# Four k-tiles of the second branch projection by seven products, two column blocks at a time

## The chip, the cores and the metric

The kernel runs on one core of a Trainium2 chip. The time is device microseconds of a whole execution, here the median of three runs. A profiled execution gives the trace. In its rows PE is TensorE's matmul, PEld its weight load, DVE VectorE, ACT ScalarE, POOL GpSimd, SP the engine that issues most loads. A line such as L109 is a line of the kernel file.

## The reference

One decoder layer on x of 256 rows and 2048 columns, all in float32:

- h = rmsnorm(x), then one projection into queries, keys and values of 16 heads of 128, and into three gates of 2048 columns each;
- three kinds of attention side by side: stick-breaking on 4 heads, block attention on 6, dilated attention on 6;
- the merge, which the change is about:

```python
merged = (gates[:, :, 0] * (flat(o_a) @ w_branch[:ea])
          + gates[:, :, 1] * (flat(o_b) @ w_branch[ea:eb])
          + gates[:, :, 2] * (flat(o_c) @ w_branch[eb:]))
x = x + merged @ w_out
```

- a second rmsnorm, a SwiGLU network of width 5632, and the residual.

## The kernel before

**Numbers in two parts.** Every float32 operand of a matmul is split into a high part in TensorE's reduced format and the remainder: `split` (L109) casts on ACT and subtracts on DVE. A product (`product`, L173 to L175) is three matmuls into the same PSUM bank: high x high, high x low, low x high. Activations are the stationary side (128 x 128), weights the moving side (128 x 512).

**Tiles.** Rows make two row tiles of 128; columns go by blocks of 512; the inner dimension by k-tiles of 128. A load fetches two k-tiles of one column block, 512 KB. Raw weights land in four `w_raw` buffers or in a pool called `gx`; their split parts lie in five pairs `w_hi` and `w_lo`. PSUM has eight banks: two of `ps`, two of `qs`, two for transposes (`tr`), and from the last gates on one each of `z` and `v`. `banks()` hands out `ps` and `qs` in turn.

**Plain and by sevens.** `project` (L133 on) multiplies k-tile after k-tile for one column block. `project_pair` (L358 on) does two column blocks at once, and for the chunks of four k-tiles in `acts.wc` it replaces eight block products (2 row tiles x 2 column blocks x 2 halves of k) by seven, as Winograd's form of Strassen's method does. The weights are then quarters b11, b12, b21, b22 of 512 KB and sums of them; the activations are four blocks and four sums of them, made by `put_sums` (four subtractions or additions, L227 to L232, and a split). The order is: form 1 into X, form 5 into Z, form 2 into Y, plain blocks of the second column block into Z and V, form 6, form 7, form 3, then the plain blocks of the first column block and form 4. With `by_banks` the bank X is copied to Y, and Z to V, on ACT; otherwise snapshots in SBUF serve. With `by_dma` the sum b12 + b22 is made by an accumulating transfer on POOL's queue, as u + b21 always is.

**The stages.** Input projection (pairs, chunks 0 and 1 by sevens), attention beside it, the branch projection, output projection, the second norm, the gate and up projection, the down projection. Work that hangs on a stage (transposes, splits, norms) is cut into steps in `stages`; `advance` runs one step at each weight block.

**The branch projection.** Column blocks c = 0 to 3, and in each the three branches with 4, 6 and 6 k-tiles, all by `project`. Behind each branch the gates, kept in DRAM, are multiplied with the banks (L988, L990) and added up (L991); their loads go by POOL (L977). After a column block, `to_m` transposes the merged rows, splits them into `m`, and for chunks 0 and 1 also makes the sums that the output projection wants. At the last branch the pools of the attention phase (`ph1`) are closed and the first output pair is begun.

**What sets the order.** A planner places the instructions of each engine, in the order in which they can start by its own timeline; those pinned by `keep_in_program_order` keep the written order. `fetch` (L106) pins loads on SP, `raw_weights` (L121) doesn't.

## Time and profile before

| | us |
|---|---|
| median of 3 runs | 1335.99 (1335.94 to 1340.19) |
| profiled execution | 1341.53 |
| its span | 1339.8 |
| TensorE busy | 1329.8 (99%) |
| VectorE busy | 1175.4 (88%) |
| ACT busy | 946.3 (71%) |
| GpSimd busy | 132.5 (10%) |
| mean granted TensorE clock | 0.999 |

A row of busy time adds up how long an engine's instructions lasted, and overlapping ones are counted once. A timeline row has start, duration, engine, line and operation, with output and inputs; in brackets stands idle time ahead of it and what ended it.

### The profile page before, as it was taken

Reading aid. Unit: us, or ns where it says so; the run is one execution under the profiler, and the core shown is the slowest. Engines: PE = TensorE matmul, PEld = TensorE weight load, DVE = VectorE, ACT = ScalarE, POOL = GpSimd, SP = SyncE. Lnnn points to the kernel's source line nnn. Section 1 sums busy time; section 2 is a strip of 40 time slices with the busy share of each in tenths; the row PEclk is TensorE's granted clock in tenths of the full one; section 3 lists DMA queues with packets and bytes.
Section 4 is the critical chain, followed back from the end, with each engine's and each line's share of the span. In section 5 each row is a group of like instructions: output and inputs, shape, how many; then the busy total and the mean of one; then the engine's idle time right before and its main releaser. Section 6 shows DMA issues by size and latency. Waiting matters only on the chain.

```text
span 1339.8 us, 17786 instructions
## 1 busy us (share of the span) xinstructions
PE 1329.8 (99%) x6237; PEld 1159.1 (87%) x6237; DVE 1175.4 (88%) x1261; ACT 946.3 (71%) x1216; POOL 132.5 (10%) x197
## 2 busy tenths in 40 slices
PE   9999999999999999999999999999999999999998
PEld 6888888888888888888888878888888888888887
DVE  7978898988888997988999979998889997998887
ACT  6786867788777776546877867777877776664563
POOL 1100110001110111110210000001000001001010
PEclk9999999999999999999999999999999999999999
DMA  9987878888788878888988799889899877789983
GB/s 356 307 281 246 264 211 255 256 271 227 264 263 282 289 230 287 299 283 278 283 296 273 255 232 272 234 263 306 278 295 272 264 226 259 244 278 299 275 270 95
DMA packets 119793, 355.75 MB, mean 266 GB/s; under 512 B 32864, under 2 KB 34584, under 8 KB 119704
## 3 DMA queue, kind: packets, MB, share of 16 engines
q1 hardware_dynamic: 77016, 277.45, 57.6%
q0 software_dynamic: 20272, 70.81, 23.2%
q10 hardware_dynamic: 22416, 6.36, 3.1%
q8 instruction: 49, 0.80, 0.2%
q14 instruction: 40, 0.33, 0.1%
HBM read 294.26 MB, written 14.70 MB: 231 GB/s over the span
## 4 chain that ended last, share of the span: by engine, by line
PE 93%; DMA 3%; issue 2%; DVE 1%; ACT 0%; SPq 0%; DVEq 0%; POOL 0%; POOLq 0%; ACTq 0%
PE qs L174 11%; PE qs L175 11%; PE qs L173 11%; PE ps L174 11%; PE ps L175 11%; PE ps L173 11%; PE z L173 4%; PE z L175 4%; PE z L174 4%; PE v L173 2%; PE v L175 2%; PE v L174 2%; DMA u<-g_raw 1%; PE tr L175 1%; PE tr L174 1%
## 5 line engine op out<-in xcount | busy, mean ns | idle before, releaser
L109 DVE TENSOR_TENSOR w_lo<-w_raw,w_hi 128x1024 fp32r<-128x1024 f32 x298 | 361.0, 1219 | 44.7 <-ACT w_hi L109 43.3
L109 ACT CAST w_hi<-w_raw 128x1024 fp32r<-128x1024 f32 x298 | 309.4, 1048 | 94.8 <-PE qs L175 28.1
L109 ACT CAST w_hi<-g_raw 128x1024 fp32r<-128x1024 f32 x220 | 227.1, 1050 | 106.7 <-PE qs L175 32.8
L109 DVE TENSOR_TENSOR w_lo<-g_raw,w_hi 128x1024 fp32r<-128x1024 f32 x220 | 262.2, 1219 | 19.5 <-ACT w_hi L109 17.1
L109 ACT CAST w_hi<-u 128x1024 fp32r<-128x1024 f32 x165 | 172.0, 1049 | 122.3 <-DVE u L1194 21.2
L109 DVE TENSOR_TENSOR w_lo<-u,w_hi 128x1024 fp32r<-128x1024 f32 x165 | 199.2, 1221 | 48.9 <-ACT w_hi L109 44.0
L174 PE MATMUL qs<-w_lo,h_hi 128*128 128x512 f32 x348 | 133.2, 383 | 3.2 <-DVE w_lo L109 3.2
L175 PE MATMUL qs<-w_hi,h_lo 128*128 128x512 f32 x348 | 132.6, 381 | 0.0
L174 PE MATMUL ps<-w_lo,h_hi 128*128 128x512 f32 x336 | 128.0, 381 | 0.5 <-DVE w_lo L109 0.5
L173 PE MATMUL qs<-w_hi,h_hi 128*128 128x512 f32 x348 | 128.1, 384 | 0.0
L175 PE MATMUL ps<-w_hi,h_lo 128*128 128x512 f32 x336 | 127.4, 380 | 0.1
L173 PE MATMUL ps<-w_hi,h_hi 128*128 128x512 f32 x336 | 123.1, 382 | 0.2 <-ACT h_hi L109 0.2
L402 POOL DMA_DIRECT2D u<-g_raw x47 | 40.9, 871 | 380.4 <-DVE w_lo L109 309.5
L174 PEld LDWEIGHTS qs<-w_lo,h_hi 128*128 128x128 f32 x348 | 66.1, 190 | 12.9 <-DVE w_lo L109 3.6
L173 PEld LDWEIGHTS qs<-w_hi,h_hi 128*128 128x128 f32 x348 | 66.1, 190 | 9.7 <-ACT sc L335 0.3
L175 PEld LDWEIGHTS qs<-w_hi,h_lo 128*128 128x128 f32 x348 | 66.1, 190 | 9.3
L174 PEld LDWEIGHTS ps<-w_lo,h_hi 128*128 128x128 f32 x336 | 63.5, 189 | 9.9 <-DVE w_lo L109 1.3
L175 PEld LDWEIGHTS ps<-w_hi,h_lo 128*128 128x128 f32 x336 | 63.5, 189 | 9.9 <-DVE h_lo L109 1.1
L173 PEld LDWEIGHTS ps<-w_hi,h_hi 128*128 128x128 f32 x336 | 63.3, 189 | 9.6 <-ACT h_hi L109 0.9
L351 DVE TENSOR_TENSOR u<-g_raw 128x1024 f32<-128x1024 f32 x47 | 57.2, 1219 | 14.5 <-DMA g_raw<-in_w_gu 11.3
L340 DVE TENSOR_TENSOR u<-u,g_raw 128x1024 f32<-128x1024 f32 x47 | 55.4, 1218 | 0.0
L396 POOL DMA_DIRECT2D g_raw<-g_raw x21 | 18.2, 864 | 254.6 <-DMA g_raw<-in_w_in 78.0
(440 smaller groups left out, 2978.1 us busy)
## 6 DMA issues: line engine op xcount, KB each, us to landing
w_raw<-in_w_in SPq DMA_DIRECT2D x103, 512.0 KB, 6.7
g_raw<-in_w_in SPq DMA_DIRECT2D x88, 512.0 KB, 6.3
g_raw<-in_w_gu SPq DMA_DIRECT2D x88, 512.0 KB, 6.0
w_raw<-in_w_gu SPq DMA_DIRECT2D x88, 512.0 KB, 6.6
w_raw<-in_w_down SPq DMA_DIRECT2D x56, 512.0 KB, 4.8
u<-g_raw POOLq DMA_DIRECT2D x51, 512.0 KB, 6.3
w_raw<-in_w_branch SPq DMA_DIRECT2D x32, 512.0 KB, 4.7
g_raw<-in_w_down SPq DMA_DIRECT2D x32, 512.0 KB, 5.2
```

Source lines behind the costliest of these rows:

```text
L109: cast, rest = nc.scalar.copy(hi, src), nc.vector.tensor_sub(lo, src, hi.bitcast(F32))
L173: nc.tensor.matmul(ps, ah, wh, start=start, stop=False, **how)
L174: nc.tensor.matmul(ps, ah, wl, start=False, stop=False, **how)
L175: nc.tensor.matmul(ps, al, wh, start=False, stop=stop, **how)
L340: tc.keep_in_program_order(nc.vector.tensor_add(d, d, a))
L351: nc.vector.tensor_add(d, a, b)
L396: nc.gpsimd.dma_start(d, a, accum_op=ALU.add)
L402: nc.gpsimd.dma_start(d, a, accum_op=ALU.add)
```

## The change

The loop over four column blocks becomes a loop over two pairs. In a pair the order is now: first branch of the second block; then `project_pair` for the second branch of both blocks, with k-tiles 4 to 7 (the first four of its six) by sevens and k-tiles 8 and 9 plain; inside it, after form 6, the first branch of the first block (`between`); then the third branch of both.

`project_pair` takes the list of plain k-tiles `ks` and the function `between`. With a single plain block per column it skips the plain blocks ahead of form 6, and the two banks of the first column block end with form 4. `by_banks` now holds for `w_branch` too.

The sums of heads 4 to 7, which the forms need, are made in place in `o_raw` at the end of the last gates, and split into a new pool `os`. For the second branch no new raw buffers are taken: the quarters b11, b12, b21, b22 lie in the slot of `h_hi` (the first norm's high parts), u and that branch's gates in the slot of `o_raw`, and the merged sums of the first pair in the slot of `h_lo`. `Slots` hands these out in order. The gates of the second branch are fetched at the beginning of a pair.

```diff
     def by_banks(w):
-        return w is w_gu or w is w_out
+        return w is not w_in
...
-        ks = [k for c in range(KT // 4) if c not in acts.wc for k in (4 * c, 4 * c + 2)]
+        ks = ks or [k for c in range(KT // 4) if c not in acts.wc for k in (4 * c, 4 * c + 2)]
+        split_at = (2, 3) if len(ks) > 2 else (0, len(ks))
...
-        rest(1, ks[2], Z, V)
+        if between:
+            between()
+        for k in ks[slice(*split_at)]:
+            rest(1, k, Z, V, stop=k == ks[-1])
...
-            rest(0, k, Y, X)
-        form(X, 4, u, False, False)
+            rest(0, k, Y, X, stop=k == ks[-1])
+        form(X, 4, u, False, len(ks) <= 2)
...
+        if k0:
+            for _ in range(2):
+                yield
+            heads_4_7 = o_raw[:, 4:8, :]
+            o_sums.put_sums(1, *(heads_4_7[:, :, t * P:(t + 1) * P] for t in range(NT)), heads_4_7)
...
-    for c in range(4):
-        ms = [half_kb() for _ in range(NT)]
-        for b, (k0, nk) in enumerate(((0, H_A), (H_A, H_B), (H_A + H_B, H_C))):
-            gt = [half_kb() for _ in range(NT)]
-            for t in range(NT):
-                nc.gpsimd.dma_start(gt[t], gate_mem[b, c, t])
-            ps = project(o, k0, w_branch, k0 * P, nk, c * NB)
...
+    def room(name):
+
+        return p1.tile([P, NH, S], F32, name=name).rearrange("p (n h) q -> p n (h q)", h=2 * NB // S)
...
+    kept = room("h_lo").rearrange("p n (t h) -> p n t h", t=NT)
+
+    for c in (0, 2):
+        if c:
+            ms = [[half_kb() for _ in range(NT)] for _ in range(2)]
+        else:
+            ms = [[kept[:, n, t] for t in range(NT)] for n in range(2)]
+        raws, other = room("h_hi"), room("o_raw")
+        gx = Slots((raws[:, 0], raws[:, 1], other[:, 0], raws[:, 2], raws[:, 3])[i].rearrange("p (k n) -> p k n", k=2) for i in range(5))
+        gts = [gates_of(1, c + n, [other[:, 2 + n, t * NB:(t + 1) * NB] for t in range(NT)]) for n in range(2)]
+        gated(0, ms[1], *branch(0, c + 1))
+        (a0, a1, _, _), _ = project_pair(o_sums, w_branch, c * NB, (c + 1) * NB, None, None, True,
+                                         lambda *b: gated(1, ms[1], gts[1], b), [H_A + 4],
+                                         lambda: gated(0, ms[0], *branch(0, c)))
+        turn.reverse()
+        gated(1, ms[0], gts[0], (a0, a1))
+        for n in range(2):
+            gt, ps = branch(2, c + n)
...
+            with behind_splits() if c + n == 3 else nullcontext():
+                gated(2, ms[n], gt, ps)
+            stages.append(to_m(c + n, ms[n]))
```

## The prediction

> **What bounds the kernel now.** I read the page's first part and its chain of waits, then busy times by stretch, then the instructions one by one where the changed stage begins and ends.

> ```profile
> span 1339.8 us, 17786 instructions
> PE 1329.8 (99%) x6237; PEld 1159.1 (87%) x6237; DVE 1175.4 (88%) x1261; ACT 946.3 (71%) x1216; POOL 132.5 (10%) x197
> PE 93%; DMA 3%; issue 2%; DVE 1%; ACT 0%; SPq 0%; DVEq 0%; POOL 0%; POOLq 0%; ACTq 0%
> ```

> TensorE is busy for 99% of the span and carries 93% of the chain that ended last, so work taken from it comes off the end, as long as the other engines keep it fed. The next fullest is VectorE, at 88%. The stage that changes is the projection of the three branches. In the timeline of TensorE it begins and ends here (columns: start, duration, engine, line, operation):

> ```profile
> 515.35 0.38 PE L173 MATMUL qs<-w_hi,o_hi 128*128 128x512 f32 x1
> ...
> 520.53 0.38 PE L173 MATMUL ps<-w_hi,o_hi 128*128 128x512 f32 x1
> ...
> 600.86 0.38 PE L173 MATMUL qs<-w_hi,m_hi 128*128 128x512 f32 x1
> ```

> The row at 515.35 is the first product of the attention output, the one at 600.86 the first of the output projection: the stage lasts 85.51 us. Between 515.35 and 520.53 lie the 24 matmuls of the first branch (4 k-tiles, 2 row tiles, 3 products each), so one costs 5.18 / 24 = 0.216 us from start to start, although its row says 0.38: each begins before the last has ended. The whole stage has 4 column blocks x 16 k-tiles x 2 x 3 = 384 of them. The chain of waits shows what else is in it:

> ```profile
> 542.06 0.87 PE tr L206 x8
> 563.66 0.87 PE tr L206 x8
> 585.26 0.87 PE tr L206 x8
> ```

> 384 x 0.216 + 3 x 0.87 = 85.55 us against 85.51: TensorE does not pause in this stage, and every matmul less is worth 0.216 us. What the other engines do meanwhile (columns: stretch, its length, then busy time and count of PE, weight loads, DVE, ACT, POOL, then clock and DMA):

> ```profile
> 515.35:600.86 85.51, 85.51 (x409) 75.06 (x408) 69.91 (x88) 45.58 (x52) 17.00 (x31) 1.00 0.87 305
> 540.00:580.00 40.00, 40.00 (x195) 35.16 (x194) 37.17 (x51) 21.63 (x28) 7.32 (x14) 1.00 0.83 277
> 601.00:641.00 40.00, 40.00 (x195) 35.16 (x194) 35.05 (x39) 24.13 (x31) 2.52 (x4) 1.00 0.79 264
> 641.00:690.00 49.00, 49.00 (x240) 43.09 (x240) 47.35 (x57) 39.62 (x61) 8.52 (x14) 1.00 0.95 301
> ```

> VectorE is busy for 69.91 of the 85.51 us, so it has 15.6 us to spare; in the two middle column blocks (540 to 580) only 2.8 of 40. After the stage it has 5.0 to spare in the 40 us of the first output pair and 1.7 in the next 49. TensorE is full in all four rows, the last with VectorE at 97%: nearly full is not yet too full.

> **What TensorE saves.** For each pair of column blocks, k-tiles 4 to 7 cost 4 x 2 blocks x 2 row tiles x 3 = 48 matmuls now; seven forms of 2 k-tiles and one row tile cost 7 x 2 x 3 = 42. Two pairs: 12 matmuls less, 12 x 0.216 = **2.6 us**. Loads do not change (four quarters replace four blocks, each 512 KB), nor do the transposes.

> [...]

> **What VectorE gets in exchange.** Its prices, again from start to start where it works without a gap:

> ```profile
> 522.71 3.50 DVE L109 TENSOR_TENSOR w_lo<-w_raw,w_hi 128x1024 fp32r<-128x1024 f32 x3 [1.28 <-ACT w_hi L109]
> ...
> 530.07 1.28 DVE L991 TENSOR_TENSOR sc<-sc 128x512 f32<-128x512 f32 x2
> ...
> 547.22 0.42 DVE L227 TENSOR_TENSOR sc<-sc 128x256 f32<-128x256 f32 x1
> 547.67 0.43 DVE L230 TENSOR_TENSOR sc<-sc 128x256 f32<-128x256 f32 x1
> ```

> Three of 1024 columns take 3.50 us with the last one's 1.22 us, so one per (3.50 - 1.22) / 2 = 1.14 us; two of 512 take 1.28 with the last one's 0.68, so one per 0.60; those of 256 follow at 0.45. Per pair the change adds three low-part splits (seven forms need seven weights, where four blocks needed four) and the two sums u = b11 + b12 and u + b22, each of 1024: 5 x 1.14 = 5.7. The differences c12 and c22, 512 each, add 2 x 0.60 = 1.2. That is 6.9 a pair and 13.8 for two. The sums of heads 4 to 7 add four of 256 and one split of 1024 once: 4 x 0.45 + 1.14 = 2.9. Together **16.7 us**. The gate products and their additions are as many as before.

> So VectorE would need 69.9 + 16.7 = 86.6 us in a stage for which TensorE needs only 85.5 - 2.6 = 82.9. The excess is **3.7 us**, more than the saving. It need not all fall on TensorE. The weight buffers hold five splits, so VectorE may enter the stage ahead and leave it with less in hand; the second chunk's sums in the merged columns (four of 0.45 and two splits of 0.60, 3.0 us) are used only in the second output pair; and 5.0 us are free right behind. Bounds on what stalls TensorE here: 0, if all of it slips into these 5.0 us, and 3.7, if none does.

> [...]

> **The start of the first pair.** Its raw quarters lie where the first norm's columns lay (h_hi), which the last product of the gates reads. That product starts just before 515.35, so these loads can only go then. They are pinned to the order of SP's queue, so what is pinned behind them waits too. What they take:

> ```profile
> L121 SPq DMA_DIRECT2D w_raw<-in_w_branch x32: 327/328/328, 500.0 to 579.2; - x32
> DMA to landing us min/median/max: 3.4/4.7/9.1
> ...
> L109 ACT CAST w_hi<-w_raw 128x1024 fp32r<-128x1024 f32 x31 | 32.4, 1050 | 35.2 <-PE ps L175 13.6 <-PE qs L175 11.3 <-DMA w_raw<-in_w_branch 8.9
> ...
> 515.55 0.69 DVE L431 TENSOR_TENSOR sc<-ps,sc 128x512 f32<-128x512 f32 x1 [0.28 <-PE ps L175]
> 516.16 1.22 DVE L109 TENSOR_TENSOR o_lo<-o_raw,o_hi 128x1024 fp32r<-128x1024 f32 x1
> ```

> The cover is the first branch of the other column block, put ahead of the pair: 5.18 us. A landing of 4.7, a cast of 1.05 and a low part of 1.22 make 6.97 us; the form's second matmul wants the low part at 5.18 + 0.22 = 5.40: 1.6 us late. At a landing of 3.4 it is 0.3 late, and work pulled forward from the other first branch (5.18 us more, free once two products of 0.60 have emptied its banks) can hide that. At 9.1 it is 6.0 late. Before this, VectorE still owes the two rows at 515.55 and 516.16 and the head sums, 0.6 + 1.14 + 2.9 = 4.6 us, and it needs u = b11 + b12 and a split right after. Bounds 0 and 6.0; I take **1.5**, near the median landing. VectorE catches up 1.5 us of its excess in this wait, so 2.2 of the 3.7 remain; I take about half, **1.2**, on TensorE, because the work that may slip (3.0 us) covers more than the remainder, but nothing orders it last.

> **What costs nothing.** ACT gets 6 casts of 1.05, one for the head sums, 4 bank copies and 4 snapshots of about 0.6, some 12 us, into a stage where it works 45.6 of 85.5 us. The accumulating transfers on POOL:

> ```profile
> 610.19 0.90 POOL L402 DMA_DIRECT2D u<-g_raw x1 [11.54 <-DVE w_lo L109]
> ...
> u<-g_raw POOLq DMA_DIRECT2D x51, 512.0 KB, 6.3
> ...
> 602.36 0.57 ACT L383 COPY qs<-qs 128x512 f32<-128x512 f32 x1 [1.85 <-PE qs L175]
> ```

> There are four more of them, 3.6 us of POOL's 68 idle ones, and each lands after about 6.3 us. Form 7 and form 4, which want them, come behind the other first branch and a plain block (24 + 12 matmuls, 7.8 us or more). A landing of 9 us would outlast that cover by 1.2. The copy of form 1's bank takes 0.57 us behind the products of form 5 (6 x 0.216 = 1.3 us). The gates come by the same 24 transfers, four in each pair earlier than now. In the second pair the quarters go into slots whose last readers stand before two third branches (2 x 36 x 0.216 = 15.6 us), so the late start does not come again.

> **The sum.** -2.6 (matmuls) + 1.5 (first quarters) + 1.2 (VectorE) = +0.1 us. The profiled execution took 1341.5 us, 1.7 more than its span; it would take 1341.6. The three timed runs have a median of 1336.0, 5.5 below it, and a highest of 1340.2; the change carries over as a difference: **1336.1 us**. With the bounds: 1336.0 - 2.6 = 1333.4 at best, and 1336.0 - 2.6 + 6.0 + 2.2 = 1341.6 at worst, since a wait of 6.0 leaves VectorE no excess and the 2.2 then stand for its own gaps.

> **Rivals.** *Clean gain.* The planner fills the start with the other first branch and spreads VectorE's excess into the 5.0 us behind: 1333.4. For it speaks the row of 641 to 690 (97% VectorE, TensorE full), and that the first output pair, which has the same 186 matmuls with one chunk by sevens, runs at 601 to 641 without a pause. Against it: that pair leaves VectorE 5.0 us free, and has no gate products (20 x 0.60 = 12 us a branch pair).

> *VectorE becomes the bound; slower.* In the second pair the columns of two merged blocks (4.2 us each: two splits, four sums, two splits) fall together with the seven forms. TensorE gives a form 1.3 us, and a form asks 1.14 us of split, in two cases another 1.14 of sum. Once the five-buffer lead has run out, each form waits for its low part. If VectorE gets no fuller than the 97% of that best row, its 86.6 us need 89.3: 3.8 us more than the stage has now. Some 1.2 us more come with a start it cannot use: 1341. Against it: the 5.0 us behind.

> *Late first quarters alone.* A landing of 9.1 us, as the slowest weight block of this stage had, and a queue held behind it: -2.6 + 6.0 = +3.4, 1339.4. Against it: the transfers ahead of it in the queue are only those of the two first branches.

> **How the numbers follow.** Forecast (1334.7 to 1338) 45%, clean gain 28%, VectorE the bound 19%, late quarters 8%. About 0.3%, 4.0 us, is what a measurement of this kernel can tell from no change. Faster by that would need more than the 2.6 us there are, and so another order of later stages: 4%. Slower by it is most of the VectorE case and a little of the late quarters: 14%. Within it: 82%. The range leaves out the far end of the slow case and takes 0.4 us below the clean gain: 1333.0 to 1341.5.

> **What would show it.** The stage holds 12 fewer wide matmuls and TensorE's busy time in it drops by 2.6 us; a gap stands before the first form of the first pair, ended by a load, a cast or a low part; VectorE's busy share of the stage rises from 82% to over 95%, and later gaps of TensorE end with low parts. I am wrong if VectorE stays under 90% busy, if the stage is over 89 or under 83 us, or if the time moves outside it.

## The result and the profile after

The changed kernel takes **1349.9 us** (median of five, 1349.57 to 1352.74), the kernel before in the same comparison 1336.2 us: a ratio of 1.0105, 95% interval 1.0094 to 1.0116. It is slower by 13.7 us. The forecast was 1336.1 in a range of 1333.0 to 1341.5, so the time lies outside it, beyond every rival.

The first part of the page of the changed kernel:

```profile
span 1347.9 us, 17777 instructions
PE 1332.2 (99%) x6225; PEld 1158.1 (86%) x6225; DVE 1190.0 (88%) x1280; ACT 956.4 (71%) x1231; POOL 135.9 (10%) x201
```

The 12 matmuls are gone (6237 to 6225), yet TensorE's busy time rose by 2.4 us, so some matmuls lasted longer. Where, TensorE's timeline of the changed kernel shows (start, duration, engine, line, operation; in brackets idle time ahead and what ended it). Its rows are the first product of the stage, the pause ahead of the pair, what comes next, and then the first product of the output projection and the first of its second pair:

```profile
516.83 0.38 PE L173 MATMUL qs<-w_hi,o_hi 128*128 128x512 f32 x1
...
522.64 0.48 PE L173 MATMUL ps<-w_hi,o_hi 128*128 128x512 f32 x1 [0.47 <-ACT w_hi L109]
525.32 0.48 PE L173 MATMUL z<-w_hi,hi 128*128 128x512 f32 x1 [2.20 <-ACT w_hi L109]
525.92 0.48 PE L174 MATMUL ps<-w_lo,o_hi 128*128 128x512 f32 x1
...
527.19 0.63 PE L175 MATMUL ps<-w_hi,o_lo 128*128 128x512 f32 x1
...
608.10 0.48 PE L173 MATMUL qs<-w_hi,m_hi 128*128 128x512 f32 x1 [1.67 <-ACT w_hi L109]
...
696.85 0.38 PE L173 MATMUL qs<-w_hi,h_0hi 128*128 128x512 f32 x1
```

In the kernel before, the row that answers to the last one is:

```profile
683.36 0.38 PE L173 MATMUL qs<-w_hi,h_0hi 128*128 128x512 f32 x1
```

From these starts and those in the prediction come three parts:

| us | before | after | difference |
|---|---|---|---|
| up to the first product of the stage | 515.35 | 516.83 | +1.5 |
| the stage | 85.51 | 91.27 | +5.8 |
| the first output pair, up to the second | 82.50 | 88.75 | +6.2 |
| the rest, by the profiled executions | 656.4 | 651.1 | -5.3 |

The first three sum to 13.5 us, nearly the whole difference of the medians. Each is read from one execution of either kernel, and the first part varies between executions (515.35 here, and 514.98 in the kernel before with more work on VectorE, which is added behind it). The last line needs a word. The profiled execution of before took 1341.5 us where the median is 1336, and most of the reason stands in its waits and its busy time by stretch (stretch, its length, then PE, weight loads, DVE, ACT, POOL, clock, DMA share and GB/s):

```profile
PE qs L174 <- DVE w_lo L109: 3.2, 1, 3.2
...
796.00:800.00 4.00, 0.79 (x5) 0.36 (x3) 3.04 (x4) 4.00 (x7) 0.00 (x0) 1.00 1.02 412
800.00:804.00 4.00, 4.00 (x12) 3.30 (x13) 4.00 (x5) 1.39 (x2) 0.00 (x0) 0.65 0.56 228
```

One wait of 3.2 us for a low part, and behind it four microseconds at a clock of 0.65, which cost about 0.35 x 4 = 1.4 us: an estimate of 4.6 us from these rows. The profiled execution after has no wait of TensorE in this last part, so the two spans differ by 8.1 us only. The differences by stage are the ones to explain.

The same view of the changed kernel, by stretch:

```profile
516.83:608.10 91.27, 86.11 (x397) 73.62 (x396) 80.51 (x101) 53.48 (x64) 19.58 (x34) 0.98 0.86 286
...
522.00:526.00 4.00, 1.22 (x4) 0.46 (x3) 3.10 (x4) 2.37 (x3) 1.11 (x3) 1.00 1.02 409
526.00:528.00 2.00, 2.00 (x6) 1.63 (x7) 2.00 (x2) 0.35 (x2) 0.31 (x1) 0.64 1.00 346
528.00:530.00 2.00, 2.00 (x6) 1.60 (x5) 1.87 (x3) 0.44 (x2) 0.57 (x1) 0.50 1.11 369
530.00:534.00 4.00, 3.29 (x14) 2.27 (x14) 2.44 (x3) 4.00 (x5) 0.92 (x2) 1.00 0.47 94
534.00:605.00 71.00, 71.00 (x339) 62.23 (x338) 67.96 (x87) 39.72 (x48) 13.61 (x24) 1.00 0.86 280
605.00:612.00 7.00, 3.63 (x18) 2.33 (x16) 4.04 (x5) 3.49 (x5) 0.44 (x1) 0.99 1.02 417
612.00:618.00 6.00, 5.30 (x13) 4.08 (x13) 6.00 (x8) 3.50 (x5) 0.45 (x1) 0.50 0.63 146
...
560.00:603.00 43.00, 43.00 (x208) 37.68 (x208) 42.99 (x59) 24.88 (x32) 8.27 (x14) 1.00 0.81 255
```

The reader sees two holes, at 522 to 526 and at 605 to 612, each followed by matmuls at half the clock (granted 0.50 from 528 to 530 and from 612 to 618; a row has 0.63 us instead of 0.38, and starts follow each other by 0.43 instead of 0.216). Between them, from 534 to 605, TensorE never stops, although VectorE is full from 560 on. VectorE's share of the stage is 80.51 / 91.27 = 88%, since the stage became longer.

**The start.** What SP, ACT and VectorE do there (rows of their timelines, changed kernel):

```profile
516.81 2.31 SPq L106 DMA_DIRECT2D h_hi<-in_w_branch  x4
...
521.54 1.05 ACT L109 CAST w_hi<-h_hi 128x1024 fp32r<-128x1024 f32 x1 [0.56 <-DMA h_hi<-in_w_branch]
524.22 1.05 ACT L109 CAST w_hi<-o_raw 128x1024 fp32r<-128x1024 f32 x1 [1.63 <-DVE o_raw L351]
...
522.90 1.23 DVE L351 TENSOR_TENSOR o_raw<-h_hi 128x1024 f32<-128x1024 f32 x1 [4.05 <-DMA h_hi<-in_w_branch]
524.05 0.69 DVE L1005 TENSOR_TENSOR h_lo<-qs,sc 128x512 f32<-128x512 f32 x1
524.65 1.22 DVE L109 TENSOR_TENSOR w_lo<-h_hi,w_hi 128x1024 fp32r<-128x1024 f32 x1
```

The first quarter lands 4.7 us after its load, as forecast, and is cast by 522.6. But VectorE's queue holds the sum u first (L351). That needs the second quarter, so VectorE idles 4.05 us up to 522.90. Behind it stands a gate product, and only then, at 524.65, comes the low part for which form 1's second matmul waits. TensorE starts that one at 525.92.

**The end.** Rows of SP's, ACT's, TensorE's and VectorE's timelines of the changed kernel, then two of the kernel before:

```profile
601.08 1.28 SPq L106 DMA_DIRECT2D g_raw<-in_w_out  x3
...
606.03 1.07 ACT L109 CAST m_hi<-tr 128x512 fp32r<-128x512 f32 x2 [8.21 <-PE tr L206]
606.99 1.06 ACT L109 CAST w_hi<-g_raw 128x1024 fp32r<-128x1024 f32 x1
...
609.22 1.22 DVE L351 TENSOR_TENSOR u<-g_raw 128x1024 f32<-128x1024 f32 x1
```

```profile
579.59 1.81 SPq L106 DMA_DIRECT2D g_raw<-in_w_out  x3
...
590.70 1.05 ACT L109 CAST w_hi<-g_raw 128x1024 fp32r<-128x1024 f32 x1 [1.54 <-PE qs L175]
...
596.24 1.22 DVE L351 TENSOR_TENSOR u<-g_raw 128x1024 f32<-128x1024 f32 x1
```

The first quarters of the output weights are loaded 21.5 us later than before (their slots overlay those of the second branch's gates). Their first cast stands on ACT behind two casts of transposed merged columns, which wait 8.21 us for TensorE's transposes. TensorE then waits for the cast (1.67 us), the low part (0.78), u's cast (0.92) and u's low part (0.70), and its clock is at 0.50 from 611.9 on.

### The profile page after: what moved, and what is told of

Its sections match the earlier page's. It is cut to its first block, busy times and chain, and to the rows that moved or that the text cites. A ratio compares the mean times of both kernels' runs of the same rounds, so it can differ in the third digit from the quotient of the medians.

```text
span 1347.9 us, 17777 instructions
## 1 busy us (share of the span) xinstructions
PE 1332.2 (99%) x6225; PEld 1158.1 (86%) x6225; DVE 1190.0 (88%) x1280; ACT 956.4 (71%) x1231; POOL 135.9 (10%) x201
## 4 chain that ended last, share of the span: by engine, by line
PE 97%; DMA 1%; DVE 1%; ACT 1%; issue 0%; SPq 0%; DVEq 0%; ACTq 0%
PE qs L173 12%; PE qs L174 12%; PE qs L175 12%; PE ps L174 11%; PE ps L175 11%; PE ps L173 11%; PE z L174 5%; PE z L175 5%; PE z L173 5%; PE v L173 3%; PE v L174 3%; PE v L175 3%; PE tr L175 1%; PE tr L174 1%; PE tr L173 1%; PE tr L206 1%
## 5 line engine op out<-in xcount | busy, mean ns | idle before, releaser
L109 DVE TENSOR_TENSOR w_lo<-w_raw,w_hi 128x1024 fp32r<-128x1024 f32 x290 | 351.9, 1221 | 36.2 <-ACT w_hi L109 35.0
L109 ACT CAST w_hi<-w_raw 128x1024 fp32r<-128x1024 f32 x290 | 301.1, 1047 | 76.1 <-PE qs L175 16.3
L109 ACT CAST w_hi<-g_raw 128x1024 fp32r<-128x1024 f32 x220 | 227.0, 1050 | 102.4 <-PE qs L175 30.7
L109 DVE TENSOR_TENSOR w_lo<-g_raw,w_hi 128x1024 fp32r<-128x1024 f32 x220 | 262.8, 1223 | 20.0 <-ACT w_hi L109 17.5
L109 ACT CAST w_hi<-u 128x1024 fp32r<-128x1024 f32 x165 | 172.1, 1049 | 116.1 <-PE qs L175 21.3
L109 DVE TENSOR_TENSOR w_lo<-u,w_hi 128x1024 fp32r<-128x1024 f32 x165 | 199.6, 1224 | 42.4 <-ACT w_hi L109 37.4
L175 PE MATMUL qs<-w_hi,h_lo 128*128 128x512 f32 x348 | 132.1, 379 | 0.0
L175 PE MATMUL ps<-w_hi,h_lo 128*128 128x512 f32 x336 | 127.4, 380 | 0.1
L173 PE MATMUL qs<-w_hi,h_hi 128*128 128x512 f32 x348 | 127.4, 382 | 0.0
L173 PE MATMUL ps<-w_hi,h_hi 128*128 128x512 f32 x336 | 123.1, 382 | 0.2 <-ACT h_hi L109 0.2
L173 PEld LDWEIGHTS qs<-w_hi,h_hi 128*128 128x128 f32 x348 | 65.7, 189 | 9.5 <-ACT sc L335 0.4
L175 PEld LDWEIGHTS qs<-w_hi,h_lo 128*128 128x128 f32 x348 | 65.8, 189 | 9.2
L175 PEld LDWEIGHTS ps<-w_hi,h_lo 128*128 128x128 f32 x336 | 63.5, 189 | 9.8 <-DVE h_lo L109 1.1
L173 PEld LDWEIGHTS ps<-w_hi,h_hi 128*128 128x128 f32 x336 | 63.3, 189 | 9.5 <-ACT h_hi L109 0.9
L351 DVE TENSOR_TENSOR u<-g_raw 128x1024 f32<-128x1024 f32 x47 | 57.4, 1223 | 12.2 <-DMA g_raw<-in_w_gu 10.2
L174 PE MATMUL ps<-w_lo,hi 128*128 128x512 f32 x116 | 44.7, 386 | 0.5 <-DVE w_lo L109 0.5
## 6 DMA issues: line engine op xcount, KB each, us to landing
w_raw<-in_w_in SPq DMA_DIRECT2D x103, 512.0 KB, 6.8
g_raw<-in_w_in SPq DMA_DIRECT2D x88, 512.0 KB, 6.2
g_raw<-in_w_gu SPq DMA_DIRECT2D x88, 512.0 KB, 6.1
w_raw<-in_w_gu SPq DMA_DIRECT2D x88, 512.0 KB, 6.4
w_raw<-in_w_down SPq DMA_DIRECT2D x56, 512.0 KB, 4.6
u<-g_raw POOLq DMA_DIRECT2D x51, 512.0 KB, 6.4
g_raw<-in_w_down SPq DMA_DIRECT2D x32, 512.0 KB, 5.0
g_raw<-g_raw POOLq DMA_DIRECT2D x26, 512.0 KB, 8.2
```

What stands on the lines that cost most here:

```text
L109: cast, rest = nc.scalar.copy(hi, src), nc.vector.tensor_sub(lo, src, hi.bitcast(F32))
L173: nc.tensor.matmul(ps, ah, wh, start=start, stop=False, **how)
L174: nc.tensor.matmul(ps, ah, wl, start=False, stop=False, **how)
L175: nc.tensor.matmul(ps, al, wh, start=False, stop=stop, **how)
L351: nc.vector.tensor_add(d, a, b)
```

## Experiments

In the texts on record, theory A is that the time lies in these two waits, each from where the change put its slots, with the half clock behind them; theory B, set against it, is VectorE's load inside the stage; theory C, formed after the first runs, is the place of the merged columns' casts in ACT's queue; theory D, formed after the second set of runs, is VectorE's load behind these waits: full from about 560 on, it comes late to the output projection. "Difference" below is the median less that of the kernel before on the same chip; "stage" and "pair" are the two parts of the table above.

### The gates of the second branch in another slot

```diff
-        gts = [gates_of(1, c + n, [other[:, 2 + n, t * NB:(t + 1) * NB] for t in range(NT)]) for n in range(2)]
+        gts = [gates_of(1, c + n, [kept[:, 2 + n, t] for t in range(NT)]) for n in range(2)]
```

> Edit: the gates of the second branch lie in the free half of the slot of h_lo, no longer in the slot of o_raw, which the first raw buffers of the output projection reuse; nothing else is changed. Theory A (two local waits, each followed by matmuls at half clock, make the loss): the output weights are issued some 10 us or more ahead of the end of the stage instead of at 601.1 us, TensorE does not wait between 605 and 613 us, the granted clock stays 1.0 there, and the time falls by about 6 us, to 1344. The start of the stage keeps its wait. Theory B (VectorE, full from 570 to 603 us, is what holds the stage back): the loads come earlier but low parts are late all the same; the time falls by at most 1 us.

1348.96 us, ratio 1.0094 (1.008 to 1.0109), difference 12.3. Stage 91.7, pair 88.1. Rows of SP and ACT:

```profile
591.11 1.60 SPq L106 DMA_DIRECT2D g_raw<-in_w_out  x3
...
605.29 1.07 ACT L109 CAST m_hi<-tr 128x512 fp32r<-128x512 f32 x2 [7.42 <-PE tr L206]
606.25 1.06 ACT L109 CAST w_hi<-g_raw 128x1024 fp32r<-128x1024 f32 x1
```

The output weights come 10 us earlier, and their cast is no earlier: it stands behind the same two casts on ACT. The slot was late, but was not what ended the wait, and theory A's 1344 did not come.

### The first pair's quarters in their own buffers

```diff
-    pgx.close()
...
-        raws, other = room("h_hi"), room("o_raw")
-        gx = Slots(...)
+        other = room("o_raw")
+        if c:
+            raws = room("h_hi")
+            gx = Slots(...)
...
+        if c == 0:
+            pgx.close()
+            m = Columns(pool(pm, "pm", "right"), "m", KT)
+            ms_sums = Both(pe0, m, WC)
         gated(1, ms[0], gts[0], (a0, a1))
```

> Edit: the five raw buffers of the first pair stay in the pool of the input projection (gx), which the merged columns take over only after that pair; the slot of h_hi is used for the second pair alone. Theory A: the first quarters are issued before the last product of the gates, the gap behind the first branch (522 to 526 us) and the half clock behind it (526.4 to 529.7 us) go, and the time falls by 6 to 8 us, to 1342 to 1344; the wait at the end stays. Theory B: without the pause at the start VectorE falls behind by as much later in the stage, and the time falls by at most 2 us.

1343.1 us, ratio 1.005 (1.0036 to 1.0063), difference 6.5. Stage 85.5, pair 88.2. TensorE's rows at the start, and its stretches:

```profile
521.36 0.38 PE L175 MATMUL qs<-w_hi,o_lo 128*128 128x512 f32 x1
521.57 0.38 PE L173 MATMUL ps<-w_hi,o_hi 128*128 128x512 f32 x1
```

```profile
520.00:524.00 4.00, 4.00 (x21) 3.44 (x19) 2.72 (x4) 3.99 (x6) 3.15 (x6) 1.00 1.07 369
...
600.00:608.00 8.00, 3.85 (x15) 2.29 (x13) 6.25 (x8) 5.52 (x8) 0.89 (x1) 1.00 0.96 365
```

Form 1 follows the first branch without a pause, at full clock, and the whole is 13.7 - 6.5 = 7.2 us better than the change, as theory A said: the place of the first quarters is shown to be what the start costs. The hole at the end is still there.

### Both

The two edits together.

> Edit: both edits together (gates apart, first pair's buffers in the input projection's pool). Theory A: neither wait is left, TensorE is full through the stage, and the time is that of the kernel before less the 12 matmuls, plus up to 1.5 us of small waits: 1333.5 to 1335.5, a ratio of 0.998 to 0.9995. Theory B: VectorE needs more than TensorE in this stage, so waits on low parts appear in the second pair or at the start of the output projection, and the time is 1339 or more.

1344.95 us, ratio 1.0059 (1.0046 to 1.0072), difference 8.3: no better than the second edit alone, and far from theory A's 1333.5 to 1335.5. With the first edit alone this says that the slot of the gates is not, by itself, the end's cause. (Its profiled execution has a pause of 2.06 us at 571, longer than any that the other kernels with these edits show there, so its stages are not compared.)

### The start's pause filled with matmuls

```diff
-        gated(0, ms[1], *branch(0, c + 1))
+        gt, ps = branch(0, c + 1)
+        if c == 0:
+            nothing = tr.tile([P, NB], F32, name="tr")
+            with tc.issue_after(last_product[0].ins):
+                for _ in range(14):
+                    nc.tensor.matmul(nothing, o.hi[:, 0, :P], o.hi[:, 0:2, :].rearrange("p k q -> p (k q)"), start=True, stop=True)
+        gated(0, ms[1], gt, ps)
```

> Edit: the changed kernel with 14 matmuls into an unused bank, behind the first branch of the first pair, where TensorE otherwise waits; their results are not read. Theory A (the clock falls because TensorE idles): the granted clock stays 1.0 from 522 to 530 us, the matmuls from 526.4 us on take 0.216 us instead of 0.427, and the stage gets 1.5 to 2 us shorter although 14 matmuls (3.0 us) are added; time 1348. Rival (the clock falls for another reason, as the load of the chip): the half clock stays, and the added work costs 0 to 3 us; time 1350 to 1353.

`last_product` holds the last matmul issued so far. 1347.17 us, ratio 1.0077 (1.0062 to 1.0093), difference 10.6: 3.1 us better than the change by the differences, with 14 matmuls more. Stage 90.2, pair 86.9. So the traces show 1.1 us of the gain in the stage. Another 1.8 lie in the pair, where the half clock lasted only from about 608 to 611 (clock 0.80 over 608 to 616) instead of from 611.9 to 618.7; nothing ties that to the added matmuls. Its row of added matmuls, and the stretch behind it:

```profile
521.75 3.35 PE L1031 MATMUL tr<-o_hi 128*128 128x512 f32 x14
```

```profile
524.00:528.00 4.00, 3.89 (x18) 2.86 (x17) 4.00 (x5) 2.54 (x3) 0.64 (x1) 1.00 1.02 392
```

The low part comes as late as before (the second product starts at 525.67, in the changed kernel at 525.92), but the clock stays at 1.00, where the changed kernel has 0.64 and 0.50 (the rows at 526 and 528 above). The 14 matmuls are what the two differ in, so at this place the half clock follows from TensorE's idling and not from what else runs at that time. Ahead of it TensorE was busy for 1.22 of 4 us in the changed kernel. By the granted clock it lasted from about 526.6 to 530.0 there (3.4 us, in which TensorE did not pause), and at the end of the stage from about 611.9 to 618.7 (6.8 us, with one pause of 0.70 us in it). With the quarters in their own buffers, 3.85 busy of 8 us (the row at 600 above) did not lower it (1.00 from 600 to 616), while 3.63 busy of 7 us in the changed kernel (the row at 605) was followed by the half clock. So the busy share alone does not tell when it falls.

### The casts of the merged columns behind the first output weights

```diff
+            if c + n == 2:
+                late_m = to_m(c + n, ms[n])
+            elif c + n == 3:
+                pin_m.append(1)
+                stages.append(late_m)
+                stages.append(to_m(c + n, ms[n]))
...
         p11 = [parts(b) for b in b11]
+        if first_out:
+            tc.keep_in_program_order(split_last[0])
+            tc.keep_in_program_order(split_last[1])
```

The columns of the third block are transposed later, and their splits are pinned behind those of the first output quarters and of u.

> Edit: the merged rows of block 2 are turned (to_m) only after the first two weight splits of the output projection have been issued, and these splits and the casts into m are pinned in that order on ACT and VectorE; the gates stay in the slot of o_raw. After e1_gates_apart, where the output weights were issued 10 us earlier and TensorE waited just as long, the theory for the end of the stage is now C: ACT's queue has the casts of the merged rows, which wait for transposes that TensorE does last, in front of the first cast of the output weights. With the order alone turned, the output weights are still issued at about 600 us behind the gates of the second branch, so the first cast waits for their landing: C expects 1.5 to 3 us less than the changed kernel, 1347 to 1348.5. If the slot didn't matter at all: 5 to 6 us less.

1350.19 us, ratio 1.0099 (1.0082 to 1.0115), difference 13.9: as slow as the change, not the 1347 to 1348.5 of theory C. Stage 89.5, pair 91.8: what the stage gains, the pair loses.

The same with the second edit (own buffers):

> Edit: first pair's raw buffers in the input projection's pool (e2_first_in_gx, 1343.1) and the merged rows of block 2 later (e6_merge_later). C: 1.5 to 5 us under e2_first_in_gx, as the output weights there were issued at 594 us, some 5 us ahead of their use: 1338 to 1341.5.

1343.96 us, ratio 1.0053 (1.0042 to 1.0065), difference 7.6. Stage 83.6, pair 90.1. It is no better than the second edit alone (6.5), where theory C gave 1.5 to 5 us less. With the first edit (gates apart):

> Edit: e6_merge_later together with the gates apart (e1_gates_apart). C, with both the slot and the order in ACT's queue needed: TensorE does not wait between the stage and the output projection, the clock stays 1.0 there, and the time is 5 to 6 us under the changed kernel: 1344 to 1345. If VectorE's load is what holds the output projection back: within 2 us of the changed kernel.

1348.85 us, ratio 1.009 (1.0075 to 1.0106), difference 12.5, within 2 us of the change, as the expectation has it for VectorE's load. With all three:

> Edit: all three: first pair's buffers in the input projection's pool, gates apart, merged rows of block 2 later. Theory C with theory A's start: no wait of TensorE above 1 us is left in the stage or at its end; the time is that of the kernel before less 2.6 us plus up to 2 us of small waits: 1334 to 1336.5 against 1336.6. If VectorE's load is a bound of its own, waits on low parts turn up elsewhere in the second pair or the first output pair and the time stays above 1339.

1343.46 us, ratio 1.0047 (1.0034 to 1.006), difference 7.1. Stage 84.4, pair 89.2. The stage is within 1.5 us of what the saving promised (82.9), and the output pair takes 6.7 us longer than before. Its stretches, a row of ACT and two of VectorE:

```profile
560.00:598.00 38.00, 37.93 (x180) 32.92 (x179) 38.00 (x54) 21.91 (x29) 6.92 (x13) 1.00 0.86 278
600.00:608.00 8.00, 6.50 (x31) 4.69 (x30) 6.81 (x10) 6.45 (x9) 0.89 (x1) 1.00 0.60 170
...
593.26 1.05 ACT L109 CAST w_hi<-g_raw 128x1024 fp32r<-128x1024 f32 x1 [0.26 <-DMA g_raw<-in_w_out]
...
597.69 1.21 DVE L109 TENSOR_TENSOR w_lo<-g_raw,w_hi 128x1024 fp32r<-128x1024 f32 x1
598.83 1.21 DVE L357 TENSOR_TENSOR u<-g_raw 128x1024 f32<-128x1024 f32 x1
```

VectorE is busy for all of the 38 us up to 598, and gets to the first low part of the output projection at 597.69 (before: 595.10). The cast that this low part needs ended at 594.3, so nothing holds it but VectorE's own queue. TensorE's pauses from 600 to 616 are 2.3 us instead of the change's 4.1, without half clock. But 2.0 us of pauses stand at 650 to 655 (a low part, a residual sum, a copy on ACT), where the changed kernel has none. Neither slot nor order was the end's only cause, theory C's 1334 to 1336.5 was missed, and this led to theory D.

### Twelve additions by accumulating transfers

```diff
                 nc.vector.tensor_mul(gt[t], ps[t], gt[t])
-                nc.vector.tensor_add(ms[t], ms[t], gt[t])
+                if by_queue:
+                    nc.gpsimd.dma_start(ms[t], gt[t], accum_op=ALU.add)
+                else:
+                    nc.vector.tensor_add(ms[t], ms[t], gt[t])
```

In the kernel with all three edits, for 12 of the 16 additions.

> Edit: e8_all_three (first pair's buffers in the input projection's pool, gates apart, block 2 merged later), and 12 of the 16 additions of gated branches (all of the second branch, those of the third in the first pair) by accumulating transfers on POOL's queue instead of VectorE: 12 x 0.60 = 7.2 us less for VectorE, no matmul changed. e8_all_three left 1343.5 us against 1336.3 of the kernel before, with VectorE busy for all of 560 to 598 us and the sum u for the output projection made only at 598.8. Theory D (once the two local waits are gone, VectorE's load is what remains): the sum u and the splits behind it come earlier, the waits between 600 and 616 us shrink from 2.3 to under 1 us, and the time falls by 3 to 5 us, to 1338.5 to 1340.5. Rival (what remains comes from the order of the output projection that the planner chose, not from the load): within 1.5 us of 1343.5.

1362.92 us, ratio 1.0202 (1.0188 to 1.0216), difference 26.5. Stage 101.0. Its longest wait in the stage (waiter, what it waited for, us, times, longest), and the row of VectorE that ends it:

```profile
PE tr L206 <- DVE sc L1017: 6.1, 1, 6.1
...
614.66 0.69 DVE L1017 TENSOR_TENSOR sc<-sc 128x512 f32<-128x512 f32 x1 [12.16 <-DMA sc<-h_lo]
```

A miss: an addition left on VectorE waits 12.16 us for the accumulating transfer ahead of it, TensorE's transposes wait for that addition, and another wait of 3.4 us stands at 582. The transfers brought waits of their own, so the run says nothing on VectorE's load.

### The kernel before, with more work on VectorE

```diff
+    def more_vector(a):
+        for n in range(2):
+            nc.vector.tensor_add(spare[:, :S], a[:, :S], a[:, S:])
...
                         nc.vector.tensor_mul(ms[t], ps[t], gt[t])
+                        more_vector(gt[t])
```

48 additions of 256 columns, whose results nobody reads.

> Edit: the kernel before, with 48 more additions of 256 columns on VectorE in the branch projection (two behind each of its 24 gate products, some 17 to 21 us, written to an unused tile); matmuls, loads, casts and buffers are as before. It measures the price of VectorE's load alone. Theory D: VectorE then needs 87 to 91 us in a stage of 85.5, and the time rises by 4 to 8 us. If the load does not matter because it slips behind the stage: at most 1.5 us more.

1340.57 us, ratio 1.0037 (1.0023 to 1.005), difference 4.1. Stage 85.5, unchanged; pair 87.2, 4.7 more. Stretches:

```profile
540.00:580.00 40.00, 40.00 (x195) 35.18 (x194) 39.86 (x66) 21.09 (x26) 5.34 (x10) 1.00 0.79 266
...
600.00:608.00 8.00, 5.82 (x19) 3.91 (x18) 6.81 (x8) 4.97 (x6) 0.89 (x1) 0.81 0.40 90
```

Without any part of the change, load on VectorE alone leaves the stage as it is, with VectorE at 39.86 of 40 us, and opens the same hole at 600 to 608, half clock included (rows of 0.63 us from 605.40 on, a clock of 0.81 over the 8 us). The run flatters theory D a little: six of the additions stand in one row directly ahead of the first low part of the output weights.

### Sevens in the first pair only

The first pair with its own buffers; column blocks 2 and 3 by the old loop.

```diff
-    for c in (0, 2):
+    for c in (0,):
...
+    for c in (2, 3):
+        ms = [half_kb() for _ in range(NT)]
+        for b in range(3):
+            gt, ps = branch(b, c)
```

> Edit: sevens in the first pair only, with its buffers in the input projection's pool (as e2_first_in_gx); blocks 2 and 3 by the loop of the kernel before. TensorE saves 6 matmuls (1.3 us); VectorE gets 6.9 + 2.9 = 9.8 us more instead of 16.7, and blocks 2 and 3 and the end of the stage are as before. Theory D: VectorE fits (69.9 + 9.8 = 79.7 of 84.2 us), the wait at the end of the stage is gone, and the time is 1335 to 1337.5. If pairs by sevens cost by their form and not by VectorE's load: about half of the loss of e2_first_in_gx, 1339 to 1340.

1338.71 us, ratio 1.0013 (1.0004 to 1.0022), difference 2.3. Stage 85.0, pair 82.5 as before. The stretch behind the stage:

```profile
600.00:608.00 8.00, 8.00 (x39) 7.03 (x38) 7.45 (x9) 3.66 (x5) 0.34 (x1) 1.00 0.57 127
```

With the second pair's load gone the hole at the end is gone. The time lies above the 1335 to 1337.5 of theory D, just under its rival's 1339 to 1340, and the pair's order is gone with its load, so the next run takes away load in the same written order.

### All three edits, without the twelve additions

```diff
-                    nc.gpsimd.dma_start(ms[t], gt[t], accum_op=ALU.add)
+                    pass
```

These lines differ from the kernel with the transfers.

> This is the kernel of e8 with 12 of its 16 additions of gated branches left out: those of the second branch in both pairs and those of the third branch in the first pair (the merged columns then lack these terms, so the output is not the reference's). TensorE's work and every wait's place stay as in e8; only VectorE loses 12 x 0.60 = 7.2 us, all of it before the last two third branches. e8 took 1343.5 us, with 84.3 in the stage and 89.2 in the first output pair, where the kernel before has 82.5. Theory D (VectorE is full from about 560 us on and arrives late with the first low parts and the first sum u of the output projection): 7.2 us less load lets it arrive that much earlier, u's sum at 592 or before instead of 598.8, the first output pair takes 82.5 to 86, and the whole 1337 to 1341 us. Rival (the planner's order of the casts, copies and low parts behind the stage, whatever the load): the pair stays at 88 to 90 and the whole at 1342 to 1345 us.

1339.44 us, ratio 1.0026 (1.0017 to 1.0035), difference 3.0. Stage 84.3, pair 85.3. Stretches and a row of VectorE:

```profile
560.00:598.00 38.00, 38.00 (x182) 33.31 (x181) 33.80 (x42) 22.37 (x27) 6.31 (x11) 1.00 0.86 287
600.00:608.00 8.00, 8.00 (x44) 6.96 (x43) 7.91 (x10) 4.57 (x8) 0.00 (x0) 1.00 0.63 147
...
594.86 1.22 DVE L357 TENSOR_TENSOR u<-g_raw 128x1024 f32<-128x1024 f32 x1
```

Against the kernel with all three edits, VectorE comes to u 4.0 us earlier, TensorE is full at 600 to 608, the pair is 3.9 us shorter and the difference 4.1 smaller; the written order is the same. That is what theory D said (its u at 592 or before was not reached), and not its rival's 1342 to 1345. The run is not load alone: without these additions the first block's transposes start at 539.45 instead of 557.41, so the work behind them moved too. The run with more work on VectorE, which adds load alone, points the same way.

No version ran faster than the kernel before.

## Why the prediction was wrong

**"What TensorE saves", right.** 12 matmuls fewer. Where both the start and the order at the end are mended, the stage takes 84.4 us, and 83.6 without the gates' edit, against 85.5: 1.1 and 1.9 of the 2.6 us show there, and are lost behind. In the changed kernel itself TensorE's busy time in the stage rose from 85.51 to 86.11 us: by the half clock (1.7 us at the start), and because a matmul ahead of a pause counts for its whole 0.38 to 0.48 us instead of 0.216.

**"The start of the first pair", the step that failed first.** It was put at 1.5 us, with 0 and 6.0 as bounds. Landing, cast and place were right (the forecast was a low part at 6.97 us behind the load; the cast ended at 522.6, 5.8 behind it, so its low part could have ended near 523.8). Two things were not in it. The step put u behind the low part, and in the queue u and a gate product came ahead, which set TensorE's second matmul to 525.92. And it charged idle time by its length alone: 8 or so matmuls behind it ran at 0.43 us instead of 0.216, another 1.7 us, and 0.71 us of further pauses followed by 532.5. Undoing the part gave 7.2 us. The forecast's own rival, "late first quarters alone", had the place and 6.0 us.

**"Work pulled forward can hide that", wrong.** Of the other first branch nothing was placed in the pause: the pair's forms 1 and 5 come first.

**"What costs nothing", the step that failed at the end.** The loads of the output weights, the slots they overlay and the casts that then queue ahead of theirs were not looked at: the step named no cover for them. The pair behind the stage lost 6.2 us. Moving the gates or the casts alone did not give it back. With both moved the pauses at the end shrink from 4.1 to 2.3 us, and then VectorE is what TensorE waits for there; some of the gain is lost again at 650 to 655.

**"What VectorE gets in exchange", near in size and wrong in place.** The page has 19 instructions and 14.6 us more for VectorE, where the sum had 16.7. All of them were charged to the stage, but the sums of heads 4 to 7 (2.9 us) were done long before it, the last of them in the changed kernel here:

```profile
484.01 1.22 DVE L109 TENSOR_TENSOR lo<-o_raw,hi 128x1024 fp32r<-128x1024 f32 x1
```

With the step's own prices that leaves 69.9 + 13.8 = 83.7 us in the stage against TensorE's 82.9, an excess of 0.8 instead of 3.7. The forecast let the first wait take 1.5 of the 3.7, put 1.2 on TensorE inside the stage and let the rest slip into 5.0 us free behind it. Inside the stage nothing stalled: 71 us without a pause with VectorE full from 560 on, and the same with extra load on the kernel before. But the free time behind was not free. The first things that the next stage wants are VectorE's, a low part and u, and u is followed by a cast and a second low part. TensorE waits for what is late there (with more work on VectorE alone 0.46 us for the low part, 0.94 for u's cast, 0.78 for u's low part). Taking away 7.2 us of additions gave 4.1 us. The prediction also took 601 to 641 for the first output pair with "the same 186 matmuls"; that is half of it, and the pair lasts to 683.36.

**The signs given.** The pause ahead of the first form, and "the time moves outside it" were seen. The stage over 89 us was named as a failure and came (91.3). VectorE at over 95% of the stage was not seen (88%). It was full where it mattered, but the pauses at both ends thinned the mean.

**What stays open.** With all edits and without the additions 3.0 us are left. By its trace 1.8 us of pauses stand at 647 to 651, in the output pair, ended by a low part, a residual sum and a copy on ACT. This place has no pause in the changed kernel, with the gates apart, or with one pair. It has 1.2 to 2.0 us in every kernel with the order's edit, but also 0.8 with the quarters in their own buffers alone and 1.3 with these and the gates apart. Taking 7.2 us of load away changed it only from 2.0 to 1.8. So the load hardly counts there, and the pinned order makes it larger without being its only cause; the cause stays open.

The first product of the stage comes 0.3 to 2.0 us later than before in most of the changed kernels, partly by a pause of 0.51 us at 495 to 499 for a low part, which every kernel with the change has and neither kernel without it, partly by waits in the first 10 us that differ from execution to execution (for one line's casts 0.2 us in the kernel before and 1.0 in the same kernel with more work on VectorE behind, 1.2 in the changed kernel). In the kernel with one pair the traces show no loss in stage or pair. Its 2.3 us by the medians are explained only as far as the stage began late (517.03), and that in the slowest of its eleven executions.

Whether the missing additions alone, without the order's edit, would mend the end wasn't run. Nor was the full load with the first low part and u placed ahead of the last gate products in VectorE's queue, which would tell its load from the order of its queue.

## What to carry to other kernels

VectorE's 5.0 us of slack behind this stage did not cover what was added, because the next stage begins with VectorE's work: with more work on VectorE alone the output pair lost 4.7 us, and without the twelve additions it got 3.9 back. So ask what TensorE wants first in the next stage, and what stands ahead of it in each engine's queue (here two casts on ACT that waited 8.21 us). Where a change hands TensorE's time to an engine that is already 93% busy in the middle of a stage (37.17 of 40 us here), price the delay at the next place where the two meet, not in the stage. And price a pause with the half clock behind it: at the start here a pause of 2.20 us had 1.7 us on top, and with matmuls without use in the pause the stage was 1.1 us shorter than with the pause.
